# Two-layer hybrid encoder: GpSimd makes the low parts of nine attention weight tiles a layer, the first A head's weights are turned by VectorE and transfers, V's second block is scaled by VectorE

## The chip, the core and the metric

The kernel runs on one core of a Trainium2 chip. The time is that of the device, in microseconds (us), from the start to the end of one execution; the median of several executions counts. The engines in the text are TensorE (PE in the profile: matrix products, and PEld, its weight loads), VectorE (DVE), ScalarE (ACT), GpSimd (POOL) and SyncE (SP), which here only starts transfers. SBUF is the on-chip memory that all of them read and write, PSUM the accumulators that TensorE writes. Each engine runs its own instructions in order.

## The reference

The kernel computes a trunk of two layers over 256 tokens (S) of width 1024 (D), all in float32:

```python
for l in range(2):
    x = x + 0.5 * swiglu(rms_norm(x, ffn1_norm[l]), ffn1_w_gate[l], ffn1_w_up[l], ffn1_w_down[l])   # width 2816
    h = rms_norm(x, mix_norm[l])
    qa, ka, va, qb, kb, vb = split(h @ w_in[l])         # 512, 128, 128, 512, 512, 512 columns
    out_a = windowed_gqa_sink(qa, ka, va, sink[l])      # 8 query heads of 64, 2 key/value heads, window +-128
    out_b = differential_attention(qb, kb, vb, lam)     # 4 heads of two softmaxes, values 128 wide
    out_b = rms_norm(out_b, diff_subln[l]) * (1 - lam_init)
    x = x + concat(out_a, out_b) @ w_out[l]
    x = x + 0.5 * swiglu(rms_norm(x, ffn2_norm[l]), ffn2_w_gate[l], ffn2_w_up[l], ffn2_w_down[l])
return rms_norm(x, final_norm)
```

Both attentions add a bias that grows with the distance (ALiBi); A's softmax has a learned sink logit in its denominator; B's weights are softmax 1 minus lambda times softmax 2.

## The kernel before

**Products in three parts.** A float32 value is split into a high part (the value cast to fp32r, a shorter float) and a low part (the value minus the high part). Each product is made of three: activations' high by weights' high, low by high, high by low. ScalarE casts the high parts, VectorE subtracts for the low ones.

**The stream of weights.** `specs` lists all weight tiles in the order of use. SP's queue brings each into one of six buffers `raw`; `emit_split(i, j)` makes the high and low tiles (both named `w`) of half j of tile i, in one of seven pairs of buffers. Tiles in the set `fine` are split in two pieces of 128x512, so that one half tile is two casts and two subtractions. `ahead` and `weights` run this some halves ahead of use. In the attention a layer has 13 tiles: 0 and 1 are the keys of B, 2 and 3 its queries, 4 the keys and values of A, 5 and 6 its queries, 7 and 8 the values of B, 9 to 12 the output projection.

**The attention (`mix`).** Its steps are written in the order: keys and queries of B, `soft_b` for heads 0 and 1, keys and values of A, `soft_b` for heads 2 and 3, queries of A, `soft_a(0)` and `soft_a(1)`, the values of B with `soft_a(2)` and `soft_a(3)` between their two weight tiles. One call of `soft_a` does two query heads of A that share one query tile, an A head pair; the prediction calls each call's work an A head, and calls 0 and 1, or 2 and 3, a pair. It makes 12 small score products on TensorE, four minima with the bias on VectorE (`negm`), four exponentials on ScalarE, and four multiplications by 1/sum (`ra`) on VectorE:

```python
w_ = e[:, t, a * 256:a * 256 + 256]
dve.tensor_scalar_mul(w_, w_, r[:, 2 * t + a:2 * t + a + 1])
```

The weights then have tokens on the partitions, and the value products need the keys there. `keys_first` turns them: per half of the keys, four 128x128 transposes on TensorE into a bank of PSUM, and one copy of 128x512 out of it, the first half by ScalarE, the second by VectorE. `aT[0]` and `aT[1]` are the turned tiles of B's heads 0, 1 and 2, 3; `pT[0..3]` are those of A's four calls. `vB` holds the values of B: each block of 128 tokens comes out of PSUM by one multiplication with the norm factor `r`, which GpSimd computes (a power).

**Another way to turn.** `Blocks` turns a tile without TensorE: `take` is a VectorE transpose within blocks of 32x32 (one for each 128 rows), `move` four transfers on SP's queue that place the blocks, `turned` the view in which the operand then lies: 32 elements in a run. Before the change only the norms use it.

**What sets the order.** Up to the values of B a scheduler orders each engine's instructions in the attention, by its own estimates and by priority (`urgent` raises it). From the products of V with the weights on (`kept[0] = True`) the engines run in the order written: the 32 products of B's values (eight take `aT[0]`, eight `aT[1]`, then the same for the second block of tokens), `values_a(0)`, the turning of A's calls 2 and 3, `norm_b`, which starts B's head norm, `values_a(1)`, the output projection. In the feed-forward parts the order is written out by hand in `ORDER`; GpSimd adds some weights to others there while transferring them.

## Time and profile before

| | us |
|---|---|
| median of 3 runs (906.02 to 906.24) | 906.07 |
| the profiled execution | 906.06 |
| its span in the profile | 904.3 |
| TensorE busy | 895.8 (99%) |
| its weight loads busy | 753.7 (83%) |
| VectorE busy | 738.9 (82%) |
| ScalarE busy | 562.0 (62%) |
| GpSimd busy | 52.8 (6%) |

The span runs from the first to the last instruction of the profile; the profiled execution's time is 1.76 us more. The granted clock of TensorE is 0.998 of full speed. Layer 0's attention lies between about 185 and 255 us of the span. In rows of the timeline the first number is the start in us and the second the time until the last of the group ended; then come engine, line (L80 for nearly all, since one helper issues them), operation, output<-inputs, shape and count. `ps` is a PSUM bank, `s` one of the 14 general buffers of 128x1024. In brackets stands a wait ahead of the row, and what ended it. In rows of groups the numbers behind the bar are busy time in us, mean ns of one, and idle time ahead.

### The profile page before, as it was taken

How to read it: one execution, taken by the hardware profiler on the slowest of the kernel's cores; microseconds unless marked ns; L12 is line 12 of the kernel's file. 1: busy time of each engine (PE TensorE's matmuls, PEld its weight loads, DVE VectorE, ACT ScalarE, POOL GpSimd, SP SyncE). 2: the span in 40 equal slices, each digit the busy share in tenths (PEclk: the TensorE clock that was granted, in tenths of full speed). 3: DMA queues.
4: the chain of work that ended last, by engine and by line, in shares of the span. 5: the costliest groups of instructions: out<-in, count | busy, mean ns of one | idle time of the engine just before them, and what ended most of it. 6: DMA issues, size and time to landing. Idle time of an engine off the chain costs nothing.

```text
span 904.3 us, 12641 instructions
## 1 busy us (share of the span) xinstructions
PE 895.8 (99%) x4514; PEld 753.7 (83%) x4514; DVE 738.9 (82%) x1110; ACT 562.0 (62%) x913; POOL 52.8 (6%) x72
## 2 busy tenths in 40 slices
PE   9999999999999999999999999999999999999997
PEld 7878888899878888888888888888998888888886
DVE  6689997879977798987768978888798768978883
ACT  6766655567746675665575664654686485665661
POOL 0411000000000010000000000000000000000001
PEclk9999999999999999999999999999999999999999
DMA  9989999766526979999769899996752478799921
GB/s 341 318 248 320 331 242 329 221 169 184 159 73 191 269 211 309 315 239 311 236 173 282 199 330 278 297 289 181 199 184 94 117 207 274 197 347 278 296 65 46
DMA packets 137664, 211.36 MB, mean 234 GB/s; under 512 B 5759, under 2 KB 56001, under 8 KB 137601
## 3 DMA queue, kind: packets, MB, share of 16 engines
q1 hardware_dynamic: 123840, 184.05, 62.0%
q0 software_dynamic: 12928, 25.46, 16.3%
q10 hardware_dynamic: 832, 1.05, 0.3%
q8 instruction: 35, 0.57, 0.3%
q14 instruction: 29, 0.23, 0.1%
HBM read 192.71 MB, written 1.05 MB: 214 GB/s over the span
## 4 chain that ended last, share of the span: by engine, by line
PE 95%; DVE 2%; ACT 2%; issue 1%; POOLq 0%; POOL 0%; DVEq 0%; ACTq 0%
PE ps L80 95%; DVE w L80 1%; ACT w L80 1%; ACT s L80 1%; DVE s L80 0%; DVE tmp L80 0%; ACT tmp L80 0%; ACT L80 0%; DVE xk L80 0%; POOLq L1225 0%; POOL rf L80 0%; DVEq L1225 0%; ACT junk L80 0%; ACTq L80 0%; DVE rf L80 0%
## 5 line engine op out<-in xcount | busy, mean ns | idle before, releaser
L80 PE MATMUL ps<-w,s 128*128 128x512 f32 (+1 forms) x2994 | 681.5, 388 | 0.4 <-DVE s L80 0.4
L80 PEld LDWEIGHTS ps<-w,s 128*128 128x128 f32 x2994 | 558.8, 188 | 116.8 <-issue 0.8
L80 DVE TENSOR_TENSOR w<-raw,w 128x1024 fp32r<-128x1024 f32 (+1 forms) x416 | 434.2, 1085 | 76.3 <-ACT w L80 72.3
L80 ACT CAST w<-raw 128x1024 fp32r<-128x1024 f32 (+1 forms) x416 | 377.3, 942 | 170.2 <-PE ps L80 146.1
L80 PE MATMUL ps<-s,w 128*128 128x256 f32 x672 | 83.8, 285 | 0.0
L80 PEld LDWEIGHTS ps<-s,w 128*128 128x128 f32 x672 | 81.7, 191 | 1.2
L80 PE MATMUL ps<-w,q 128*128 128x512 f32 x288 | 69.3, 390 | 0.1
L80 PEld LDWEIGHTS ps<-w,q 128*128 128x128 f32 x288 | 53.9, 188 | 11.7 <-issue 0.5
L80 ACT ACTIVATE s<-s,gcol 128x256 fp32r<-128x256 f32 (+1 forms) x64 | 27.0, 497 | 42.4 <-DMA s<-s 42.4
L80 DVE STREAM_TRANSPOSE s<-s 128x512 f32<-128x512 f32 (+1 forms) x48 | 46.2, 1000 | 0.0
L80 POOL DMA_DIRECT2D raw<-in_ffn_w_up_dram x16 | 21.0, 1314 | 398.1 <-DVE ms L80 145.0
L80 ACT CAST s<-s 128x256 fp32r<-128x256 f32 x88 | 29.3, 403 | 11.1 <-DMA s<-s 11.0
L80 ACT ACTIVATE s<-s,negm 128x256 f32<-128x256 f32 x64 | 31.9, 500 | 6.6 <-DVE negm L80 6.3
L80 DVE TENSOR_TENSOR s<-s,s 128x256 fp32r<-128x256 f32 x88 | 31.5, 419 | 4.7 <-ACT s L80 4.7
L80 ACT ACTIVATE tmp<-ps,r 128x512 f32<-128x512 f32 (+1 forms) x40 | 24.9, 643 | 13.3 <-PE ps L80 12.6
L80 ACT CAST q<-tmp 128x512 fp32r<-128x512 f32 x20 | 12.3, 617 | 30.0 <-DVE tmp L80 30.0
L80 DVE TENSOR_TENSOR xk<-xk,ps 128x512 f32<-128x512 f32 x21 | 14.3, 682 | 18.1 <-PE ps L80 18.1
L80 DVE SCALAR_TENSOR_TENSOR s<-s,gcol,s 128x256 fp32r<-128x256 f32 x40 | 16.8, 483 | 10.7 <-ACT s L80 10.6
L80 PE MATMUL ps<-w,v 128*128 128x512 f32 x96 | 23.4, 390 | 0.5 <-DVE w L80 0.5
L80 DVE STREAM_TRANSPOSE s<-xk 128x512 f32<-128x512 f32 x20 | 22.0, 1101 | 0.7
L80 ACT ACTIVATE tmp<-tmp,r 128x512 f32<-128x512 f32 x8 | 5.8, 724 | 26.1 <-DVE tmp L80 26.1
L80 PEld LDWEIGHTS ps<-w,v 128*128 128x128 f32 x96 | 17.9, 188 | 4.6 <-DVE w L80 0.9
(117 smaller groups left out, 419.4 us busy)
## 6 DMA issues: line engine op xcount, KB each, us to landing
raw<-in_ffn_w_down_dram SPq DMA_DIRECT2D x44, 1024.0 KB, 8.2
raw<-in_ffn_w_gate_dram SPq DMA_DIRECT2D x39, 1024.0 KB, 5.7
raw<-in_ffn_w_up_dram SPq DMA_DIRECT2D x39, 1024.0 KB, 7.1
raw<-in_ffn_w_up_dram POOLq DMA_DIRECT2D x16, 1024.0 KB, 9.4
s<-s SPq DMA_DIRECT2D x120, 128.0 KB, 3.0
raw<-in_w_in_dram SPq DMA_DIRECT2D x14, 1024.0 KB, 6.4
raw<-in_ffn_w_gate_dram POOLq DMA_DIRECT2D x8, 1024.0 KB, 9.6
raw<-in_ffn_w_gate_dram SPq DMA_DIRECT2D x8, 512.0 KB, 4.7
```

What stands on the lines that cost most here:

```text
L80: ins = issue(*a, **k)
```

## The change

1. `slow` names tiles 2 to 10 of each layer's attention. Their 36 low pieces of 128x512 are subtracted by GpSimd instead of VectorE.
2. A's first call, `soft_a(0)`, is multiplied by 1/sum on ScalarE instead of VectorE, and is turned by `keys_turned(0)`: two VectorE transposes and four transfers instead of eight TensorE transposes and two copies. Its tile is then read in runs of 32 elements.
3. The copies of `aT[1]` are both VectorE's, instead of one by ScalarE and one by VectorE.
4. The second block of `vB` comes out of PSUM by VectorE instead of ScalarE.
5. `norm_b` starts ahead of `values_a(0)`.

```diff
-    fine = {2, 3}
+    fine, slow = {2, 3}, set()
...
-            dve.tensor_tensor(l_, r_, f(h_), op=ALU.subtract)
+            (pool if i in slow else dve).tensor_tensor(l_, r_, f(h_), op=ALU.subtract)
...
+        slow.update(mixed + i for i in (2, 3, 4, 5, 6, 7, 8, 9, 10))
...
-                    dve.tensor_scalar_mul(w_, w_, r[:, 2 * t + a:2 * t + a + 1])
+                    if c in (0,):
+                        act.mul(w_, w_, r[:, 2 * t + a:2 * t + a + 1])
+                    else:
+                        dve.tensor_scalar_mul(w_, w_, r[:, 2 * t + a:2 * t + a + 1])
...
-        def keys_first(pick):
+        def keys_first(pick, copies=(act.copy, dve.tensor_copy)):
...
-                (act.copy if kc == 0 else dve.tensor_copy)(out_[:, kc], tsl)
+                copies[kc](out_[:, kc], tsl)
...
+        def keys_turned(c):
+
+            turn = Blocks(by_block=False)
+            for t in range(2):
+                turn.take(p_a[c][:, t], t)
+            turn.move()
+            return turn.turned().rearrange("p (a k) y j -> p a k y j", a=2)
...
-            return keys_first(lambda kc, i: a_b[2 * hp + i // 2][:, i % 2, kc * P:(kc + 1) * P])
+            return keys_first(lambda kc, i: a_b[2 * hp + i // 2][:, i % 2, kc * P:(kc + 1) * P],
+                              [dve.tensor_copy] * 2 if hp else (act.copy, dve.tensor_copy))
...
             if k0 == 0:
+                pT = [keys_turned(0)]
                 p_a += [soft_a(2, qA1[0]), soft_a(3, qA1[1])]
         with urgent():
-            for t in range(2):
-                act.activation(vB[:, t], vsl[t], AF.Copy, scale=norm.r[:, t:t + 1])
+            act.activation(vB[:, 0], vsl[0], AF.Copy, scale=norm.r[:, 0:1])
+            dve.tensor_scalar_mul(vB[:, 1], vsl[1], norm.r[:, 1:2])
         aT.append(keys_first_b(1))
-        pT = [keys_first_a(c) for c in range(2)]
+        pT.append(keys_first_a(1))
...
-                        pe.matmul(o[j][f0, 0:S], lhsT=vA[:, kc, f0], rhs=pT[2 * cp + j][:, kc, a * 256:a * 256 + 256],
+                        pe.matmul(o[j][f0, 0:S], lhsT=vA[:, kc, f0], rhs=pT[2 * cp + j][:, a, kc],
...
+        normed = norm_b()
+        next(normed)
         values_a(0)
         pT += [keys_first_a(c) for c in (2, 3)]
-        normed = norm_b()
-        next(normed)
```

VectorE at the end of layer 0's softmaxes, before: `es`, `ra` and the `s` that `ra` multiplies belong to `soft_a(2)` and `soft_a(3)`, `w<-raw` is a low piece, and `s_450` is `aT[1]`; the other copies are A's turned tiles.

```order
L80 TENSOR_TENSOR es_2466<-negm_2457,snk 128x4
L80 TENSOR_TENSOR w_2523<-raw_2087,w_2522 128x512
L80 TENSOR_TENSOR es_2500<-negm_2491,snk 128x4
L80 TENSOR_TENSOR w_2523<-raw_2087,w_2522 128x512
L80 COPY s_450_2550<-ps_2557 128x512
L80 TENSOR_TENSOR ra_2469<-den_a_1673,es_2466 128x4
L80 COPY s_453_2563<-ps_2570 128x512
L80 RECIPROCAL ra_2469<-ra_2469 128x4
L80 COPY s_456_2576<-ps_2583 128x512
L80 TENSOR_SCALAR s_435_2456<-s_435_2456,ra_2469 128x256 x4
```

The same place of VectorE in the changed kernel, where `v` is `vB`'s second block and `s_452` is `aT[1]`:

```order
L80 TENSOR_TENSOR es_2508<-negm_2499,snk 128x4
L80 TENSOR_TENSOR ra_2477<-den_a_1673,es_2474 128x4
L80 TENSOR_TENSOR ra_2511<-den_a_1673,es_2508 128x4
L80 RECIPROCAL ra_2477<-ra_2477 128x4
L80 RECIPROCAL ra_2511<-ra_2511 128x4
L80 TENSOR_SCALAR s_437_2464<-s_437_2464,ra_2477 128x256
L80 TENSOR_SCALAR v_2401<-ps_2403,r_1787 128x512
L80 TENSOR_SCALAR s_437_2464<-s_437_2464,ra_2477 128x256 x3
L80 TENSOR_SCALAR s_443_2498<-s_443_2498,ra_2511 128x256 x4
L80 TENSOR_TENSOR w_2531<-raw_2087,w_2530 128x512 x2
L80 COPY s_452_2558<-ps_2559 128x512
L80 COPY s_452_2558<-ps_2565 128x512
```

VectorE's one copy of `aT[1]` stood ahead of the multiplications of `soft_a(2)` and `soft_a(3)`; now it has two, and both stand behind all eight of these, `vB`'s second block and two low pieces.

GpSimd from the last feed-forward transfer before layer 0's attention, in the changed kernel; `r` is the attention's norm factor:

```order
L80 DMA raw_720<-in_ffn_w_gate_dram 128x4x512
L80 TENSOR_TENSOR w_1675<-raw_1465,w_1674 128x512 x2
L80 TENSOR_TENSOR w_1681<-raw_1465,w_1680 128x512 x2
L80 TENSOR_TENSOR w_1687<-raw_1524,w_1686 128x512 x2
L80 TENSOR_TENSOR r_1787<-ms_1784,mhalf 128x2
L80 TENSOR_TENSOR w_1807<-raw_1524,w_1806 128x512 x2
L80 TENSOR_TENSOR w_1827<-raw_1578,w_1826 128x512 x2
```

Before, `r` came right behind the transfer, and nothing but `rb` of `norm_b` followed in the attention; now six low pieces stand ahead of `r`, and 30 between `r` and `rb`.

TensorE ahead of the value products of B, before; `ident` marks a transpose, `s_412` and `s_418` are the weights of A's calls 0 and 1:

```order
L80 MATMUL ps_2557<-ident,s_384_2133 128x128 x2
L80 MATMUL ps_2557<-ident,s_389_2162 128x128 x2
L80 MATMUL ps_2564<-ident,s_412_2334 128x128 x4
L80 MATMUL ps_2570<-ident,s_412_2334 128x128 x4
L80 MATMUL ps_2577<-ident,s_418_2368 128x128 x4
L80 MATMUL ps_2583<-ident,s_418_2368 128x128 x4
L80 MATMUL ps_2593<-v_2401,s_422_2388 128x128 x4
L80 MATMUL ps_2593<-v_2401,s_450_2550 128x128 x4
```

And now:

```order
L80 MATMUL ps_2565<-ident,s_384_2133 128x128 x2
L80 MATMUL ps_2565<-ident,s_389_2162 128x128 x2
L80 MATMUL ps_2572<-ident,s_418_2368 128x128 x4
L80 MATMUL ps_2578<-ident,s_418_2368 128x128 x4
L80 MATMUL ps_2588<-v_2401,s_422_2388 128x128 x4
L80 MATMUL ps_2588<-v_2401,s_452_2558 128x128 x4
```

The eight transposes of A's first call are gone, and so there is less between the transposes into `aT[1]`'s banks and the products that read it.

More of the change, by code (lines that the diff above doesn't have):

```diff
@@ L1004, in keys_first @@
                     pe.transpose(tsl[:, i * P:(i + 1) * P], pick(kc, i), ident)
-                (act.copy if kc == 0 else dve.tensor_copy)(out_[:, kc], tsl)
+                copies[kc](out_[:, kc], tsl)
             return out_
+        def keys_turned(c):
[4 more added lines that the diff above has]
+            return turn.turned().rearrange("p (a k) y j -> p a k y j", a=2)
         def keys_first_b(hp):
-            return keys_first(lambda kc, i: a_b[2 * hp + i // 2][:, i % 2, kc * P:(kc + 1) * P])
+            return keys_first(lambda kc, i: a_b[2 * hp + i // 2][:, i % 2, kc * P:(kc + 1) * P],
+                              [dve.tensor_copy] * 2 if hp else (act.copy, dve.tensor_copy))
         def keys_first_a(c):
-            return keys_first(lambda kc, i: p_a[c][:, i % 2, (i // 2) * 256 + kc * P:(i // 2) * 256 + (kc + 1) * P])
+            t_ = keys_first(lambda kc, i: p_a[c][:, i % 2, (i // 2) * 256 + kc * P:(i // 2) * 256 + (kc + 1) * P])
+            return t_.rearrange("p k (a y j) -> p a k y j", a=2, j=32)
         aT = [keys_first_b(0)]
```

## The prediction

> **What bounds the kernel now.** I read the page first, then the waits of TensorE and the chain, and then the order of time of layer 0's attention, where every edit lies.

> ```profile
> span 904.3 us, 12641 instructions
> PE 895.8 (99%) x4514; PEld 753.7 (83%) x4514; DVE 738.9 (82%) x1110; ACT 562.0 (62%) x913; POOL 52.8 (6%) x72
> PE ps L80 <- DVE tmp L80: 1.4, 1, 1.4
> 76.94 816.92 PE ps L80 x4155
> ```

> TensorE is busy for all but 8.5 us. Its longest wait is 1.4 us, at the start, and the chain is one unbroken piece of TensorE work from 76.94 us to 893.86. The profiled execution took 906.06 us, 1.76 more than its span and level with the median of 906.07. So relief of another engine is worth nothing by itself. The time falls by the TensorE work that goes, and rises by every wait that the change puts into that piece. The other engines have little room there: the timeline shows VectorE with hardly a gap from 200 to 250 us.

> **TensorE work that goes.**

> ```profile
> 207.23 0.50 PE L80 MATMUL ps<-s,q 64*128 64x256 f32 x4
> 211.57 1.45 PE L80 MATMUL ps<-s,q 64*128 64x256 f32 x20
> 215.17 1.69 PE L80 MATMUL ps<-s,q 64*128 64x256 f32 x24
> 228.70 0.50 PE L80 MATMUL ps<-s,q 64*128 64x256 f32 x4
> 244.37 2.78 PE L80 MATMUL ps<-ident,s 128*128 128x128 f32 x24
> 246.99 3.74 PE L80 MATMUL ps<-v,s 128*128 128x128 f32 x32
> 250.65 1.95 PE L80 MATMUL ps<-s,vA 128*64 128x256 f32 x16
> ```

> The 24 transposes before B's value products take 246.99 - 244.37 = 2.62 us, 0.109 each. Eight of them, the first A head's, go: 0.87 us. The new order also issues two groups of 24 score products in one piece that are now cut into 4 and 20: 0.50 + 1.45 - 1.69 = 0.26 each, 0.5 together. That is 1.37 us a layer and 2.74 us for both; the second layer repeats the first. With nothing else this gives 903.3 us. The value products of A then read half of their moving operand in runs of 32 elements instead of 256. No row shows TensorE reading so. I take nothing; if these 8 of 16 took twice their 0.12 us it would be 1.0 us a layer.

> **The wait that comes: B's second weight tile.** The products at 246.99 need both blocks of V at once and, after the first 8 of 32 (3.66 / 32 = 0.114 each, so 0.91 us later), the tile of B's heads 2 and 3. In the changed kernel they could start at 246.99 - 1.37 = 245.62, and would need that tile's first half at 246.53 and its second at 246.76. Now ScalarE copies one half and VectorE the other, and VectorE's copy stands ahead of the last A heads' scaling:

> ```profile
> 231.34 0.48 DVE L80 CUSTOM_DVE_ANT_0 s<-ps,distA,nsnk 128x256 f32<-128x256 f32 x1
> 237.75 2.19 DVE L80 TENSOR_SCALAR s<-s,ra 128x256 f32<-128x256 f32 x8
> 239.86 0.48 DVE L80 CUSTOM_DVE_ANT_0 s<-ps,distA,nsnk 128x256 f32<-128x256 f32 x1
> 245.66 0.68 DVE L80 COPY s<-ps 128x512 f32<-128x512 f32 x1
> 230.84 0.58 ACT L80 COPY s<-ps 128x512 f32<-128x512 f32 x1
> 231.87 0.51 ACT L80 ACTIVATE s<-s,negm 128x256 f32<-128x256 f32 x1 [0.45 <-DVE negm L80]
> 237.12 0.28 ACT L80 ACTIVATE es<-es 128x4 f32<-128x4 f32 x2
> 237.31 1.12 ACT L80 CAST w<-raw 128x512 fp32r<-128x512 f32 x2
> 242.37 0.67 ACT L80 ACTIVATE v<-ps,r 128x512 f32<-128x512 f32 x1
> 190.54 1.71 ACT L80 ACTIVATE s<-s,gcol 128x256 fp32r<-128x256 f32 x4 [5.89 <-DMA s<-s]
> 36.98 2.05 DVE L80 STREAM_TRANSPOSE s<-s 128x512 f32<-128x512 f32 x2
> ```

> In the new order both copies are VectorE's and stand behind the whole softmax of A heads 2 and 3, V's second block and two halves of a low part. I follow the chain in two pieces.

> First piece, from the first A pair's score minimum to the second's. Without VectorE's low parts ahead of it the first minimum could start when its scores are there: 228.70 - 0.26 + about 1.0 for the first twelve products and their latency, 229.4. Then: 0.53 to the first exponential (231.34 to 231.87); eight exponentials at 0.49 a start (3.93) and a copy (0.47); two small exponentials and two casts (1.24); the four new multiplications by 1/sum on ScalarE, as the 190.54 row (1.71); VectorE's two 32x32 transposes that wait for them (2.05); half a low part (0.6). Together 10.5 us, so the second pair's minimum starts at 239.9. Now it starts at 239.86: what the low parts free, the new steps in the chain use up.

> Second piece, from 239.9: 0.5 to the exponentials, 3.93 for eight and 0.57 for V's first block between them (5.0); small exponentials (0.28) and VectorE's small operations (0.37); one multiplication (0.26), V's second block (0.6), seven more multiplications (1.85; eight take 2.19), two halves of low parts (1.2), the copy (0.68): 10.24 us. The second copy adds 0.6. The halves land at 250.1 and 250.75. V's second block lands at 246.5, inside the same wait. TensorE needs the second half at 246.76: it waits 4.0 us a layer.

> Without anything more the sum is 906.06 + 2 x 4.0 - 2.74 = 911.3 us.

> **GpSimd's low parts and VectorE.**

> ```profile
> L80 DVE TENSOR_TENSOR w<-raw,w 128x512 fp32r<-128x512 f32 x22 | 14.3, 685 | 0.9 <-ACT w L80 0.7
> L80 DVE SCALAR_TENSOR_TENSOR s<-s,rc 128x256 f32<-128x256 f32 x8 | 3.4, 480 | 0.0
> L80 DVE TENSOR_TENSOR q<-tmp,q 128x512 fp32r<-128x512 f32 x3 | 2.1, 685 | 0.0
> L80 DVE TENSOR_TENSOR s<-tmp,s 128x512 fp32r<-128x512 f32 x2 | 1.3, 683 | 0.0
> L80 DVE SCALAR_TENSOR_TENSOR rc<-rc,nlam,den_b 128x2 f32<-128x2 f32 x4 | 0.8, 213 | 0.0
> L80 DVE TENSOR_TENSOR s<-tmp,s 128x256 fp32r<-128x256 f32 x1 | 0.4, 408 | 0.0
> L80 POOL TENSOR_TENSOR xk<-xk,s 128x512 f32<-128x512 f32 x2 | 2.6, 1300 | 45.4 <-ACT tmp L80 45.4
> 42.56 0.90 DVE L80 TENSOR_TENSOR q<-tmp,q 128x512 fp32r<-128x512 f32 x1 [0.69 <-ACT q L80]
> 43.52 2.36 DVE L80 TENSOR_TENSOR w<-raw,w 128x1024 fp32r<-128x1024 f32 x2
> 42.47 0.45 POOL L80 TENSOR_TENSOR distB<-distB 128x128 f32<-128x128 f32 x1
> L80 POOL TENSOR_TENSOR distB<-distB x2: 449/688/927, 42.5 to 45.3; 128x128 f32<-128x128 f32 x2
> ```

> The first six rows are VectorE's from 200 to 231 us. A half low part of 128x512 takes VectorE 0.685 us (0.6 to the next start), and took GpSimd 1.30 in the nearest row. There are 36 halves a layer, 46.8 us of GpSimd, from 185.5 on.

> The two work against each other. At 42.56 VectorE's q, which reads two SBUF tiles, started while GpSimd ran a product of two SBUF tiles, and took 0.90 us instead of 0.69. The other such product of GpSimd, at 45.3, met VectorE's low part of the 43.52 row and took 0.93 instead of 0.45. In the first case VectorE lost 0.21 us to a product that had begun 0.09 us earlier: GpSimd held it for 0.31 of its 0.45, all but 0.14. By that a half low part holds VectorE's two-input operations for up to 1.16 us.

> [...] With 1.30 for 1.16 as the hold the estimate would be about 3 us above mine.

> Between 200 and 231 us 18 such operations stay with VectorE (8 + 3 + 2 + 4 + 1). One that arrives at any time while GpSimd works waits half of 1.16, 0.58; one that arrives behind another, with GpSimd in line, waits the whole. GpSimd holds 36 x 1.16 = 42 us of some 60, so a mean of 0.4 is the low end; 0.85 is the high one; I take 0.7: 12.6 us. What VectorE is spared there is 21 halves (one of the 22 is cut by the window's edge) at 0.6, also 12.6. So the first A minimum comes where it comes now, at 231.3, and not at 229.4: 1.9 us later, and TensorE waits for the q and scores ahead of it. Two more such waits in the pieces above, q's second pair and a low half, add 1.4. That is 3.3 us a layer (0.8 at a mean of 0.4, some 6 at 0.85), and 7.3 with the 4.0.

> **The sum.** 906.06 + 2 x 7.3 - 2.74 = 917.9; I say 918.0 us.

> **What stays hidden.**

> ```profile
> 185.51 3.66 DVE L80 TENSOR_TENSOR w<-raw,w 128x512 fp32r<-128x512 f32 x6
> 194.10 0.73 POOL L80 TENSOR_TENSOR r<-ms,mhalf 128x2 f32<-128x2 f32 x1 [68.78 <-DVE ms L80]
> 198.68 0.59 PE L80 MATMUL ps<-dg,ones 128*128 128x256 f32 x2
> s<-s SPq DMA_DIRECT2D x120, 128.0 KB, 3.0
> 245.76 0.37 SPq L186 DMA_DIRECT2D raw<-in_ffn_w_gate_dram  x1
> ```

> GpSimd's r, on which the whole attention waits, now stands behind six low halves: 6 x 1.30 = 7.8 us from 185.51 is 193.3, just ahead of r at 194.10, and r's first user on TensorE comes at 198.68. Covered; were the halves 2 us each, r would come at 197.5 and about 1 us would show. The turned tile's four transfers land 3.0 us after the transposes, some 7 us before A's value products. On SP's queue they stand ahead of one weight load, issued at 245.76 now; the transposes are done by then. Cost nothing; that load is five tiles ahead of its use, so a slip of a few us stays hidden too.

> **The rivals.**
> No contention (0.16): the two rows above have other causes or other sizes, GpSimd runs beside VectorE, and only the copy's wait is left: 911.3 us. Against it stands that both engines' rows show the loss at the same moment, each against the other.

> Faster (0.10): the copies of B's second tile land by 246.8 all the same, because VectorE gets 4 us ahead in the attention, and only the saved TensorE work counts: 903.3 us. It needs the second pair's minimum to start by about 236, ahead of the end of its own scores in the present trace, so little speaks for it. It decides when the second copy lands before 246.76.

> No change (0.03): the wait is as small as the saving, 1.4 us a layer.

> GpSimd becomes the bound (0.07): at 1.9 us a half, as the 45.3 row doubled, V's eight halves come slower than the 1.43 us in which TensorE uses one up, fall 3.8 us behind, and TensorE waits for low parts: 918.0 + 2 x 3.8 = 925.6 us. For it speaks that VectorE's operations hold GpSimd up as well; against it the six tiles of lead.

> **How the numbers follow.** The forecast case has 0.64. Its ends are 906.06 + 2 x 4.8 - 2.74 = 912.9 at a mean wait of 0.4, and 906.06 + 2 x 10.0 - 2.74 = 923.3 at 0.85. The range reaches down to the case without contention with an error of 0.8 us a layer in its chain, 909.5, and up to 924. The faster case and most of the GpSimd case are left out. A measurement of this kernel tells 0.2%, 1.8 us, from no change. Faster has 0.10, the same 0.03, slower 0.87.

> **What would show it.** In the changed profile TensorE's waits should name VectorE before the products of V with B's tiles, 3 to 6 us a layer, with two VectorE copies side by side just ahead of their second group. A further 2 to 4 us should lie at the first A pair's scores. Low halves on GpSimd should take about 1.3 us each and up to half more, and VectorE's two-input operations of the attention should be longer than now, up to about 1.8 us, while those that read PSUM keep their length. Transposes should fall by 16. If VectorE's two-input operations keep their length, the contention step is wrong. If TensorE has no wait before B's value products, the chain is wrong. If it waits for GpSimd, the third rival holds.

## The result, and the profile after

The changed kernel takes 926.5 us (median of 4 runs, 925.32 to 927.19), the kernel before 906.05 on the same chip: 1.0223 times as long, interval 1.0211 to 1.0236. The forecast was 918.0 in a range of 909.5 to 924.0. The sign was right; the size was not: 20.4 us were added, where 12 were forecast.

The head of the page of the changed kernel, and TensorE's waits (engine and tile that wait, engine and tile waited for; us in total, times, longest us):

```profile
span 925.4 us, 12626 instructions
PE 903.1 (98%) x4498; PEld 760.3 (82%) x4498; DVE 730.2 (79%) x1036; ACT 561.5 (61%) x915; POOL 151.2 (16%) x144
PE ps L80 <- DVE s L80: 5.8, 3, 2.7
PE ps L80 <- ACT q L80: 3.3, 2, 1.7
PE ps L80 <- DVE v L80: 3.1, 2, 1.6
PE ps L80 <- DVE q L80: 2.1, 2, 1.1
PE ps L80 <- DVE tmp L80: 1.4, 1, 1.4
```

The profiled execution took 927.19 us, 21.1 more than the one before. The waits are 16.0 us with a small one that is not shown, and were 2.3: 13.7 of the 21.1. The other 7.3 are in TensorE's busy time, 903.1 for 895.8, although it has 16 products fewer. Where they come from shows in the timeline of TensorE in layer 0's attention:

```profile
229.72 0.39 PE L80 MATMUL ps<-s,q 64*128 64x256 f32 x2 [1.66 <-ACT q L80]
231.18 2.72 PE L80 MATMUL ps<-s,q 64*128 64x256 f32 x22 [1.08 <-DVE q L80]
233.83 1.97 PE L80 MATMUL ps<-ident,s 128*128 128x128 f32 x8
235.45 6.70 PE L80 MATMUL ps<-w,s 128*128 128x512 f32 x24
243.69 5.74 PE L80 MATMUL ps<-w,s 128*128 128x512 f32 x24
249.26 1.91 PE L80 MATMUL ps<-ident,s 128*128 128x128 f32 x16
251.01 0.39 PE L80 MATMUL ps<-v,s 128*128 128x128 f32 x2
252.95 0.94 PE L80 MATMUL ps<-v,s 128*128 128x128 f32 x6 [1.56 <-DVE v L80]
256.59 5.33 PE L80 MATMUL ps<-v,s 128*128 128x128 f32 x24 [2.70 <-DVE s L80]
261.86 1.95 PE L80 MATMUL ps<-s,vA 128*64 128x256 f32 x16
```

Two things are to be seen. There are two pairs of waits: 1.66 and 1.08 us ahead of A's first scores, for the two parts of q, and 1.56 and 2.70 ahead of B's value products, for V's second block and for the copies of B's second tile. And behind each pair the same products take longer: 24 products with V's weights take 6.70 us at 235.45 and 5.74 at 243.69; 24 of B's value products take 5.33, where 32 took 3.74 before, 2.8 for 24. The stretches of 2 us there say why (columns: busy time and count of PE, PEld, DVE, ACT and POOL, then the granted clock of TensorE, the transfers' share, GB/s):

```profile
228.00:230.00 2.00, 0.34 (x3) 0.19 (x2) 1.31 (x4) 1.11 (x3) 2.00 (x2) 1.00 0.00 0
232.00:234.00 2.00, 2.00 (x19) 1.78 (x18) 1.35 (x7) 1.39 (x4) 2.00 (x3) 0.50 0.93 362
238.00:240.00 2.00, 2.00 (x11) 1.64 (x10) 0.62 (x4) 0.71 (x3) 0.01 (x1) 1.00 0.63 238
258.00:260.00 2.00, 2.00 (x11) 2.00 (x11) 0.49 (x1) 0.60 (x1) 0.00 (x0) 0.50 1.02 386
```

The granted clock is halved for 6.83 us at each pair in layer 0, from within the second wait on, and for 3.41 and 6.83 us in layer 1. These 23.9 us hold 4.7 us in which TensorE stood idle; of the rest one half is lost, 9.6 us. The busy time says the same. Of the 2.74 us of work that was to go, 2.3 went: the 16 transposes and, in each layer, 0.26 for one group of 24 scores; the second group was to come in one piece and came as 2 and 22, with a wait between them. The work that stayed took 7.3 + 2.3 = 9.6 us longer.

VectorE from 200 to 231 us, the groups that answer to those of before (busy us, mean ns), and GpSimd's low pieces of the whole program:

```profile
L80 DVE SCALAR_TENSOR_TENSOR s<-s,rc 128x256 f32<-128x256 f32 x8 | 8.6, 1118 | 0.1
L80 DVE TENSOR_TENSOR q<-tmp,q 128x512 fp32r<-128x512 f32 x3 | 4.5, 1494 | 0.7 <-ACT q L80 0.7
L80 DVE SCALAR_TENSOR_TENSOR rc<-rc,nlam,den_b 128x2 f32<-128x2 f32 x4 | 2.4, 608 | 0.1
L80 DVE CUSTOM_DVE_ANT_0 s<-ps,distB 128x256 f32<-128x256 f32 x16 | 5.8, 415 | 0.1
L80 POOL TENSOR_TENSOR w<-raw,w 128x512 fp32r<-128x512 f32 x72 | 98.1, 1399 | 124.6 <-ACT w L80 68.0 <-DVE xk L80 56.6
```

VectorE's operations with two inputs in SBUF went from 480 to 1118 ns and from 685 to 1494, even the one of 128x2 from 213 to 608. The minima, which read PSUM, kept their length (421 before, 415 now).

### The profile page after: what moved, and what is told of

It reads as the page before. It is cut to its first block, busy times and chain, and to the rows that moved or that the text cites. A ratio compares the mean times of both kernels' runs of the same rounds, so it can differ in the third digit from the quotient of the medians.

```text
span 925.4 us, 12626 instructions
## 1 busy us (share of the span) xinstructions
PE 903.1 (98%) x4498; PEld 760.3 (82%) x4498; DVE 730.2 (79%) x1036; ACT 561.5 (61%) x915; POOL 151.2 (16%) x144
## 4 chain that ended last, share of the span: by engine, by line
PE 87%; DVE 9%; ACT 2%; issue 1%; POOLq 0%; POOL 0%; DVEq 0%; ACTq 0%
PE ps L80 87%; DVE s L80 5%; DVE w L80 1%; ACT s L80 1%; DVE q L80 1%; DVE tmp L80 1%; DVE rc L80 1%; ACT w L80 1%; DVE ra L80 0%; ACT q L80 0%; ACT tmp L80 0%; DVE v L80 0%; ACT v L80 0%; DVE xk L80 0%; POOLq L1240 0%
## 5 line engine op out<-in xcount | busy, mean ns | idle before, releaser
L80 PE MATMUL ps<-w,s 128*128 128x512 f32 (+1 forms) x2994 | 683.3, 389 | 0.4 <-DVE s L80 0.4
L80 PEld LDWEIGHTS ps<-w,s 128*128 128x128 f32 x2994 | 560.3, 188 | 117.3 <-issue 0.8
L80 ACT CAST w<-raw 128x1024 fp32r<-128x1024 f32 (+1 forms) x416 | 376.0, 941 | 162.6 <-PE ps L80 137.2
L80 DVE TENSOR_TENSOR w<-raw,w 128x1024 fp32r<-128x1024 f32 (+1 forms) x344 | 387.3, 1167 | 71.5 <-ACT w L80 68.9
L80 POOL TENSOR_TENSOR w<-raw,w 128x512 fp32r<-128x512 f32 x72 | 98.1, 1399 | 124.6 <-ACT w L80 68.0
L80 POOL DMA_DIRECT2D raw<-in_ffn_w_up_dram x16 | 21.0, 1314 | 408.3 <-DVE ms L80 153.7
L80 PE MATMUL ps<-s,w 128*128 128x256 f32 x672 | 83.0, 284 | 0.0
L80 PEld LDWEIGHTS ps<-s,w 128*128 128x128 f32 x672 | 81.5, 192 | 0.8
L80 PE MATMUL ps<-w,q 128*128 128x512 f32 x288 | 69.3, 390 | 0.0
L80 PEld LDWEIGHTS ps<-w,q 128*128 128x128 f32 x288 | 54.0, 188 | 11.6 <-issue 0.4
L80 ACT ACTIVATE s<-s,gcol 128x256 fp32r<-128x256 f32 (+1 forms) x64 | 27.0, 497 | 43.0 <-DMA s<-s 43.0
L80 DVE STREAM_TRANSPOSE s<-s 128x512 f32<-128x512 f32 (+1 forms) x52 | 50.4, 1008 | 0.0
L80 ACT CAST s<-s 128x256 fp32r<-128x256 f32 x88 | 29.3, 402 | 14.2 <-DMA s<-s 14.2
L80 DVE TENSOR_TENSOR s<-s,s 128x256 fp32r<-128x256 f32 x88 | 31.5, 418 | 7.9 <-ACT s L80 7.9
L80 ACT ACTIVATE s<-s,negm 128x256 f32<-128x256 f32 x64 | 31.8, 498 | 9.6 <-DVE negm L80 9.3
L80 ACT ACTIVATE tmp<-ps,r 128x512 f32<-128x512 f32 (+1 forms) x40 | 24.8, 642 | 13.3 <-PE ps L80 12.7
L80 DVE SCALAR_TENSOR_TENSOR s<-s,gcol,s 128x256 fp32r<-128x256 f32 x40 | 16.8, 483 | 19.1 <-ACT s L80 18.9
L80 ACT CAST q<-tmp 128x512 fp32r<-128x512 f32 x20 | 12.3, 616 | 29.0 <-DVE tmp L80 29.0
L80 POOL DMA_DIRECT2D raw<-in_ffn_w_gate_dram x8 | 10.3, 1286 | 117.5 <-DVE w L80 117.5
L80 DVE TENSOR_TENSOR q<-tmp,q 128x512 fp32r<-128x512 f32 x20 | 20.1, 1004 | 9.7 <-ACT q L80 9.7
L80 DVE TENSOR_TENSOR xk<-xk,ps 128x512 f32<-128x512 f32 x21 | 14.3, 679 | 16.4 <-PE ps L80 16.4
L80 PE MATMUL ps<-w,v 128*128 128x512 f32 x96 | 23.4, 391 | 0.3 <-DVE w L80 0.3
## 6 DMA issues: line engine op xcount, KB each, us to landing
s<-s SPq DMA_DIRECT2D x128, 128.0 KB, 3.2
```

What stands on the lines that cost most here:

```text
L80: ins = issue(*a, **k)
```

## The experiments

My theory after the result: GpSimd's subtractions hold up VectorE, the scheduler's new order puts the copies of B's second tile late, and every wait of TensorE that this makes is followed by work at half the clock. The rivals: the loss is in the turned tile and the copies, or TensorE's products are slower for another cause than its standing idle.

**All low parts back on VectorE (dve_low).** The rest of the change stays.

```diff
-        slow.update(mixed + i for i in (2, 3, 4, 5, 6, 7, 8, 9, 10))
```

> The changed kernel with all low parts back on VectorE; the rest of the change stays. Theory (GpSimd's low parts lengthen VectorE's two-input operations, the late copies of B's second tile add a wait, and each wait is followed by TensorE work at a lower clock): the waits at A's first scores are gone, VectorE's two-input operations keep 0.48 and 0.69 us. VectorE has 2.15 us more than before in front of the second copy, so TensorE waits 1.7 us a layer there, loses about 1.5 to the clock, and saves 1.37: about 910 us. Rival (the loss is in the turned tile and the copies, not in GpSimd): waits of 4 us or more stay and the time is 918 us or more.

Measured: 906.15 us, 0.9999 times before, interval 0.999 to 1.0009. The whole loss hangs on the GpSimd step. TensorE waits 0.63 us a layer for the second copy, not 1.7, and the clock stays up (1.0 in the run's mean):

```profile
246.72 1.28 PE L80 MATMUL ps<-v,s 128*128 128x128 f32 x10
248.63 2.72 PE L80 MATMUL ps<-v,s 128*128 128x128 f32 x22 [0.63 <-DVE s L80]
```

That I expected more has a cause in the order. With the low parts on VectorE, the scheduler puts both copies ahead of the multiplications by 1/sum; with them on GpSimd it puts them behind. The step that I saw as a relief of VectorE also chose the bad place.

**Only the low parts to GpSimd (low_only).** The kernel before with the line above added, and the subtraction on GpSimd for these tiles.

> The kernel before with only the 36 low pieces a layer moved to GpSimd. Theory: the waits at A's first scores are those of the changed kernel, 2.7 us a layer, with about 3 us a layer of lower clock behind them; VectorE's copy of B's second tile now stands behind the multiplications, for up to 1 us of wait: 906 + 2 x (2.7 + 3 + 0.5) = 918 us. Rival (GpSimd's work costs little, the copies and the turned tile cost the rest): under 909 us.

Measured: 919.33 us, 1.0143 times before (1.0126 to 1.016). Alone the step costs 13.0 us. The time is near the 918 expected, but partly by luck: the waits are 8.5 us longer in all than before, where 6.4 were expected, and TensorE's busy time 4.8, where 6 were expected.

```profile
230.55 0.39 PE L80 MATMUL ps<-s,q 64*128 64x256 f32 x2 [1.11 <-ACT q L80]
232.02 2.23 PE L80 MATMUL ps<-s,q 64*128 64x256 f32 x22 [1.09 <-DVE q L80]
255.04 2.72 PE L80 MATMUL ps<-v,s 128*128 128x128 f32 x22 [1.57 <-DVE s L80]
L80 DVE SCALAR_TENSOR_TENSOR s<-s,rc 128x256 f32<-128x256 f32 x8 | 8.6, 1121 | 0.1
```

Its parts do not add up: 13.0 alone, nothing for the rest alone, 20.4 together. Late as VectorE then is, the turned tile and V's block come on top of the wait for the copies, and behind these longer waits (1.56 and 2.70 us) the clock was at 0.50. In low_only, behind 0.55 us for V's block and 1.57 for the copies, the 22 products take 2.72 us, as they do in dve_low behind 0.63.

**Only the turned tile (turn_only).** The kernel before with `act.mul` for A's first call, `keys_turned(0)`, and the operand's view.

> The kernel before with only A's first call scaled by ScalarE and turned by VectorE and transfers. Theory: VectorE has 0.95 us more ahead of its copy of B's second tile, TensorE waits about 0.5 us a layer there and saves 1.37, so 904.5 us, or 905.5 if the short wait also lowers the clock. Rival (reading the turned tile in runs of 32 slows A's value products by 1 us a layer or more): those products take over 2.4 us in place of 1.95, and the time is 906 us or more.

Measured: 912.15 us, 1.0064 times before (1.0049 to 1.0079). Neither theory had this. The turned tile's two transposes delay the second pair's minima, so ScalarE's exponentials, and V's second block stands behind some of these on ScalarE:

```profile
248.17 0.95 PE L80 MATMUL ps<-v,s 128*128 128x128 f32 x6 [1.86 <-ACT v L80]
249.32 4.38 PE L80 MATMUL ps<-v,s 128*128 128x128 f32 x24 [0.20 <-ACT s L80]
253.64 1.95 PE L80 MATMUL ps<-s,vA 128*64 128x256 f32 x16
```

2.06 us of waits and 4.38 - 2.8 = 1.6 by which the 24 products are longer, less 0.87: 2.8 a layer, 5.6 of the 5.9 measured. In dve_low VectorE takes that block out of PSUM and the wait for it is gone; that this move alone does it is not shown, since dve_low also has both copies on VectorE and `norm_b` earlier. The last row settles one point: A's value products still take 1.95 us with runs of 32.

**TensorE kept busy in the waits (warm).** The changed kernel with:

```diff
+        def fill(n):
+            for _ in range(n):
+                pe.transpose(osl[1][:, 0:P], ident, ident)
+        fill(14)
         for t in range(2):
             for h in range(HB):
+                if t == 0 and h == 2:
+                    fill(24)
```

> The changed kernel with filler transposes on TensorE, into a bank that is not yet in use: 14 ahead of B's value products and 24 ahead of those that need B's second tile, 4.1 us inside the waits there. They change no result. Theory (the slower products behind a wait come from the clock that falls while TensorE stands idle): the 24 products behind the wait take 2.8 us in place of 5.3, the granted clock stays near 1.0 there, and the time falls by about 5 us to 921.5 us though the fillers do no useful work. Rival (the products are slower from another cause, such as where their operands come from): they stay at 5.3 us and the time stays at 926.5 us or rises.

Measured: 923.35 us, 1.0185 times before (1.017 to 1.02); 3.1 us less than the changed kernel with 76 products more.

```profile
253.37 2.78 PE L80 MATMUL ps<-ident 128*128 128x128 f32 x24
256.24 3.32 PE L80 MATMUL ps<-v,s 128*128 128x128 f32 x24
256.00:258.00 2.00, 1.80 (x14) 1.46 (x13) 1.38 (x3) 0.19 (x1) 0.00 (x0) 1.00 0.62 123
```

The 24 products take 3.32 us in place of 5.33, at a clock of 1.00 in place of 0.50. The operands are the same, so it was the idle time that lowered the clock there. From the first filler to the last value product it is 8.8 us a layer, where the changed kernel takes 10.8 from the first value product. The gain in all is 3.1 us, not 5: the 24 products still take 0.5 us over 2.8, and what the waits at A's scores cost, where there are no fillers, varies without a change there (the 22 scores behind them took 2.72 and 1.62 us in the two layers of the changed kernel, 2.36 and 2.72 here).

**Made waits (gaps, gaps2).** The kernel before with a pause ahead of B's value products and of the output projection's second half:

```diff
+    z = const.tile([P, 256], F32, name="z")
...
+    def pause(bank_, n):
+        for i in range(2):
+            pe.transpose(bank_[:, 0:P], z[:, 0:P], ident)
+            if i == 0:
+                for _ in range(n):
+                    pool.memset(z, 0.5)
...
+        pause(osl[1], (2, 8)[l])
...
+        pause(accs[1][1], (4, 12)[l])
```

That is gaps; gaps2 has (5, 7) and (6, 10).

> The kernel before with a made wait of TensorE at two places of each layer: a transpose, so many memsets of 128x256 on GpSimd that wait for it (2, 4, 8, 12), and a transpose that waits for these, into a bank not yet in use; the results are not touched. The places are ahead of B's value products (2 in layer 0, 8 in layer 1) and ahead of the output projection's second half (4 in layer 0, 12 in layer 1). Theory (the clock falls after a wait): behind the short waits, under 0.7 us, the products keep their length; behind those of 1.5 us and more they are slower for some us, and 1 to 3 us are lost on top of each. Rival (the slower products of the changed kernel have another cause): the time grows by the waits alone, and the products behind them take what they take in the kernel before.

> The kernel with made waits once more, with 5 and 7 memsets ahead of B's value products and 6 and 10 ahead of the output projection's second half, which gives waits of about 2.1, 2.8, 2.6 and 3.9 us. Theory (the clock halves once TensorE has stood idle long enough, between 2.0 and 3.1 us in one piece by the first run with made waits): the granted clock stays at 1.0 behind 2.1 us and is 0.5 for some 3 to 6 us behind 3.9; the two between tell where the change lies. Rival (the loss grows evenly with the wait): some loss behind each.

Measured: 923.65 us (2 runs, 1.0188 times before, 1.017 to 1.0207) and 924.69 (one run). First the value products of gaps behind 0.80 and 3.14 us, then those of gaps2 behind 1.99 and 2.74, with its wait of 2.33 between them, and four stretches of 3.41 us of gaps2, two at the wait of 1.99 and two at that of 2.33:

```profile
248.49 3.74 PE L80 MATMUL ps<-v,s 128*128 128x128 f32 x32
698.44 0.37 PE L80 MATMUL ps<-ident,z 128*128 128x128 f32 x1 [3.14 <-POOL z L80]
698.60 5.36 PE L80 MATMUL ps<-v,s 128*128 128x128 f32 x32
```

```profile
249.12 0.33 PE L80 MATMUL ps<-ident,z 128*128 128x128 f32 x1 [1.99 <-POOL z L80]
249.28 5.37 PE L80 MATMUL ps<-v,s 128*128 128x128 f32 x32
275.17 0.33 PE L80 MATMUL ps<-ident,z 128*128 128x128 f32 x1 [2.33 <-POOL z L80]
701.14 6.53 PE L80 MATMUL ps<-v,s 128*128 128x128 f32 x32
246.19:249.60 3.41, 1.42 (x13) 1.19 (x12) 3.23 (x12) 2.20 (x7) 1.64 (x5) 1.00 0.85 253
249.60:253.01 3.41, 3.41 (x18) 3.41 (x17) 1.07 (x4) 0.00 (x0) 0.00 (x0) 0.50 0.14 55
270.08:273.49 3.41, 2.76 (x13) 2.00 (x11) 2.43 (x4) 1.96 (x2) 0.47 (x2) 1.00 0.16 63
273.49:276.90 3.41, 1.73 (x8) 1.47 (x9) 3.33 (x3) 0.13 (x1) 1.40 (x5) 1.00 0.22 42
```

Behind 0.80 us the 32 products take 3.74, as in the kernel before; behind 1.99 they lose 1.6 us, behind 2.74 2.8, behind 3.14 1.6. The waits of 3.81 us (gaps2) and 4.54 (gaps) are followed by 3.4 and 6.0 us of work at half the clock, a loss of 1.7 and 3.0. But behind 2.33 us, and behind 1.96 in gaps, the clock stayed at 1.00. No one length of a wait separates the two cases here. The expectation of one such length did not hold, nor did that of a loss which grows with the wait.

More is seen when the granted clock of the changed kernel is read closely. While there is work left, it falls four times, at 230.72, 254.61, 688.10 and 708.58 us, and stays at 0.50 for 6.83, 6.83, 3.41 and 6.83 us. The last three of these stretches begin 7, 134 and 140 times 3.413 us behind the first, so all the changes of the clock there lie on one grid of 3.41 us. The trace read in the windows of this grid, the one ahead of each fall and those at half the clock:

```profile
227.31:230.72 3.41, 1.14 (x9) 0.73 (x7) 2.73 (x4) 2.52 (x7) 3.41 (x4) 1.00 0.12 13
230.72:234.13 3.41, 2.95 (x24) 2.73 (x25) 2.67 (x10) 2.60 (x7) 3.41 (x3) 0.50 0.84 295
234.13:237.55 3.42, 3.42 (x13) 3.03 (x12) 3.42 (x12) 3.41 (x14) 3.42 (x3) 0.50 0.43 119
251.20:254.61 3.41, 1.13 (x8) 0.75 (x7) 3.14 (x13) 1.84 (x7) 0.00 (x0) 1.00 0.01 2
254.61:258.02 3.41, 1.43 (x6) 1.33 (x7) 3.12 (x6) 0.00 (x0) 0.00 (x0) 0.50 0.28 43
258.02:261.44 3.42, 3.42 (x18) 3.42 (x18) 0.69 (x1) 0.60 (x1) 0.00 (x0) 0.50 0.69 263
684.69:688.10 3.41, 1.79 (x24) 1.56 (x24) 2.72 (x6) 3.19 (x6) 3.41 (x4) 1.00 0.56 167
688.10:691.51 3.41, 3.41 (x16) 2.98 (x13) 3.41 (x10) 2.81 (x10) 3.41 (x3) 0.50 0.43 153
705.17:708.58 3.41, 1.37 (x10) 0.98 (x8) 2.90 (x12) 2.08 (x7) 0.00 (x0) 1.00 0.02 7
708.58:711.99 3.41, 1.20 (x5) 1.10 (x6) 3.35 (x7) 0.00 (x0) 0.00 (x0) 0.50 0.18 22
711.99:715.41 3.42, 3.42 (x18) 3.42 (x18) 0.69 (x1) 0.60 (x1) 0.00 (x0) 0.50 0.80 285
```

What came next went with TensorE's busy time in the window. The four windows ahead of a fall hold 1.14, 1.13, 1.79 and 1.37 us of it; every other window of this grid at full clock, up to 920 us, holds 2.29 or more, and the clock stayed up behind it. At half the clock, the windows with 2.95, 1.43 and 1.20 us busy were followed by another at half, the four that were busy throughout by the full clock. In gaps2 a window with 1.42 us was followed by half the clock, and one with 1.73 was not, so the busy time alone does not settle what lies near 1.75.

The rows fit this. The wait of 1.99 us lay inside one window and left 1.42 us busy; the end of a window cut that of 2.33 into 0.65 and 1.68. The wait of 2.74 still ran when the clock fell (its mean from 700 to 702 us is 0.54), and the loss of 2.8 us is that of two windows; the 1.6 behind the longer wait of 3.14 is that of one. So waits of 1.96 to 3.14 us cost from nothing to 2.8 us beyond their length here, by where they fell in these windows, and no kernel here chose that.

**GpSimd's work without relief (pool_read).** The kernel before; GpSimd subtracts the same 36 pieces a layer into a scratch tile while VectorE makes them as well.

```diff
             dve.tensor_tensor(l_, r_, f(h_), op=ALU.subtract)
+            if i in slow:
...
+                pool.tensor_tensor(d_, r_, f(h_), op=ALU.subtract)    # d_: scratch
```

> The kernel before, where GpSimd makes the 36 low pieces a layer of the changed kernel a second time, into a scratch tile that nobody reads; VectorE still makes all of them, in nearly the order of before. Theory (GpSimd's subtractions hold VectorE's two-input operations): these take 1.1 us and more in place of 0.48 and 0.69, VectorE, full as it is, falls behind by 10 to 30 us a layer, and the time is 930 us or more. Rival (the engines do not hold each other up; the loss comes from the new order): VectorE's operations keep their length and the time stays under 910 us.

Measured: 968.88 us, 1.0686 times before (1.0668 to 1.0704). VectorE from 200 to 250 us, and GpSimd:

```profile
L80 DVE TENSOR_TENSOR w<-raw,w 128x512 fp32r<-128x512 f32 x21 | 28.9, 1420 | 0.0
L80 DVE CUSTOM_DVE_ANT_0 s<-ps,distB 128x256 f32<-128x256 f32 x16 | 5.7, 414 | 0.0
L80 POOL TENSOR_TENSOR junk<-raw,w 128x512 f32<-128x512 f32 x72 | 111.7, 1552 | 163.8 <-ACT w L80 150.0 <-issue 9.3
```

The order is nearly that of before, so the 62.7 us are the two engines' hold on each other and what follows from it, TensorE's waits (the longest 5.4 us) and the lower clock (0.88 on average from 190 to 260 us): 685 ns became 1420, and the minima, which read PSUM, stayed at 414.

**The copies ahead (copies_first).** The changed kernel with priority for the turning of B's second tile:

```diff
-        aT.append(keys_first_b(1))
+        with urgent():
+            aT.append(keys_first_b(1))
```

> The changed kernel with its low parts on GpSimd, and a higher priority for the turning of B's second tile: VectorE's two copies of it now stand ahead of the multiplications by 1/sum, V's second block still among them. Theory (waits and a lower clock behind each): the 2.70 us of wait for the copies are gone, the wait for V's second block stays at 1 to 2 us, the waits and the lower clock at A's first scores stay as they are: 926.5 - 2 x (2.7 + about 1) = 919 us. Rival (the loss is all in GpSimd's contention, the place of the copies is of no account): within 2 us of 926.5.

Measured: 916.94 us, 1.0116 times before (1.0102 to 1.013), 9.6 under the changed kernel. The wait for the copies is gone, that for V's block stays. Behind it the same 30 products take 3.62 us in layer 0 and 5.24 in layer 1, 1.6 longer:

```profile
252.48 3.62 PE L80 MATMUL ps<-v,s 128*128 128x128 f32 x30 [1.55 <-DVE v L80]
701.64 5.24 PE L80 MATMUL ps<-v,s 128*128 128x128 f32 x30 [2.04 <-DVE v L80]
```

So the place of the copies and what followed from it were nearly half of the loss. At A's first scores of layer 0 the waits are the same as in the changed kernel (1.73 and 1.08 for 1.66 and 1.08), but the 24 products behind take 5.70 us in place of 6.70, since the clock was low for about 3.4 us there (means of 0.97, 0.50, 0.68 and 1.00 in the four stretches of 2 us from 230 on) and not for 6.83.

**Fewer low parts on GpSimd (s11, half11), and none between the copies (low_last).** The three try for a version that beats both kernels.

```diff
 s11
-        slow.update(mixed + i for i in (2, 3, 4, 5, 6, 7, 8, 9, 10))
+        slow.update(mixed + i for i in (11,))
 half11: the same for the second half of tile 11 alone
 low_last: no GpSimd; the second half of tile 11 is split behind the turning of B's second tile
-            w = weights()
+            w = weights(held=k0 == 4)
...
+        i_v = w.i
         aT.append(keys_first_b(1))
+        kept[0] = True
+        ahead(2 * i_v + 1 + HALVES)
+        kept[0] = False
```

> The changed kernel with another choice of tiles for GpSimd: only the third tile of the output projection (number 11), whose four low pieces stand among VectorE's last steps of the softmaxes, where hardly a two-input operation is left to hold up. Theory (GpSimd costs where VectorE has two-input operations, and helps where it has none): VectorE's copies of B's second tile come 2 us earlier than with all low parts on VectorE, the wait of 0.63 us a layer there is gone, and TensorE keeps the 0.87 us a layer of the eight transposes: 906.2 - 1.7 = 904.5 us. Rival (any low part on GpSimd costs more than it frees): 907 us or more.

> As s11, but GpSimd makes only the second half (two low pieces a layer) of that weight tile. In s11 the first half fell beside the four multiplications by 1/sum, which took 3.22 us in place of 1.15; the second half falls beside VectorE's work on PSUM. Theory (GpSimd holds VectorE's operations from SBUF to SBUF, not those that read PSUM): the multiplications take 1.15 us again, V's second block and both copies land as TensorE needs them, the wait of 0.63 us a layer that was left with all low parts on VectorE is gone: 906.2 - 2 x 0.6 to 0.9 = 904.7 us. Rival (any piece on GpSimd here costs what it frees): 906 us or more.

> As dve_low (all low parts on VectorE, the rest of the change stays), with the second half of tile 11 split behind the turning of B's second tile, so that VectorE's two copies of it follow each other and the two low pieces stand behind them. Theory (with VectorE undisturbed, the 0.63 us of wait for the second copy is the low piece that stands between the copies): the wait is gone and TensorE keeps the 0.87 us a layer of the eight transposes: 906.2 - 2 x 0.6 = 905.0 us, or 904.5 with the whole saving. Rival (another wait of the same length is next in line): 906 us or more.

Measured: s11 906.62 us (1.0004, 0.9995 to 1.0013), half11 906.69 (1.0008, 0.9999 to 1.0017), low_last 905.44 (0.9994, 0.9984 to 1.0003). The first two missed. First VectorE's four multiplications by 1/sum in dve_low and in s11, then, in half11, one addition of 128x4:

```profile
238.45 1.15 DVE L80 TENSOR_SCALAR s<-s,ra 128x256 f32<-128x256 f32 x4
```

```profile
237.79 3.22 DVE L80 TENSOR_SCALAR s<-s,ra 128x256 f32<-128x256 f32 x4
```

```profile
245.84 1.07 DVE L80 TENSOR_TENSOR es<-negm,snk 128x4 f32<-128x4 f32 x1
246.84 1.87 DVE L80 COPY s<-ps 128x512 f32<-128x512 f32 x3
```

Two low pieces on GpSimd lengthened the multiplications, which have one tile from SBUF as input, by 2.1 us, and TensorE waits 0.65 us for V's second block, which stands behind them. In half11 the addition, 0.17 us in dve_low, met GpSimd's piece and took 1.07, and the copies stood behind it; TensorE still waits 0.58 us for them. In low_last, as expected, TensorE's list has no wait over 0.2 us left but the 1.4 at the start; the 0.7 us that it is ahead is not clear of the measurement. No version here is measurably faster than the kernel before.

## Why the prediction was wrong

**The step that failed** is the first line of the sum: "The time falls by the TensorE work that goes, and rises by every wait that the change puts into that piece." TensorE's remaining work was counted at the length that it has in the profile before, where the granted clock is 1.00 as long as TensorE works. That profile has no wait of over 1.4 us ahead of a product, so no row of it shows a product behind a longer one. It does show that the clock falls, at its end, behind the last product, which ends at 898.15:

```profile
900.00:902.00 2.00, 0.00 (x0) 0.00 (x0) 0.82 (x2) 0.66 (x1) 0.00 (x0) 0.57 0.36 125
```

It fell at 900.27, 2.1 us after the last product; the mean of 0.998 comes from there. The prediction did not read it, and put what follows a wait at nothing. The term measures 9.6 us. With it, with the waits of 13.7 and with the 2.3 us of work that went the sum is 906.06 + 13.7 + 9.6 - 2.3 = 927.1; the profiled execution took 927.19. That idle time is the cause is shown by warm and by the made waits.

**The waits were nearly right in size.** 14.6 us were forecast, 13.7 came. The wait at A's first scores was forecast at 3.3 us a layer and is 2.74; the one ahead of B's value products at 4.0 and is 4.26. Its inside is other than forecast: 1.56 us of it are for V's second block, which was to land inside the wait for the copies. That the second came out so close is partly luck. VectorE's first copy landed at 256.5 us, 3.1 later than forecast (250.1 + 3.3), mainly because the chain's first piece took 13.3 us and not 10.5: ScalarE's cast in it waited 1.35 us for TensorE, and the transposes stood behind four multiplications of the other call. TensorE, at its lower clock, came to the value products 2.1 us later than forecast (251.0, for 245.6 + 3.3), and the two delays largely cancel.

**Contention was right**, and so was its mean: the operations of 200 to 231 us lost (1118 - 480) x 8 + (1494 - 685) x 3 + (608 - 213) x 4 ns = 9.1 us on 15 of the 18, 0.61 each, for the 0.7 taken. That operations with two inputs in SBUF are held came as forecast, and so did the unchanged length of the minima, which read PSUM (421 ns before, 415 in the changed kernel). Too narrow was my reading that only the former are held: the multiplications by 1/sum, with one such input, took 3.22 us in place of 1.15 in s11.

**The chain was right for a part of the reason only.** The copies stood where the order showed them. That they stand there because of the GpSimd step, and not of the step that gives both to VectorE, came out with dve_low.

**What was called hidden was hidden.** TensorE waits for GpSimd nowhere, so r and the low parts come in time; the transfers of the turned tile and its runs of 32 cost nothing (1.95 us for the 16 products as before); 16 transposes went. Of the two groups of 24 scores the first came in one piece of 1.69 us; the second did not, as its second half of q came late.

**The rivals.** No contention is refuted by pool_read, GpSimd as the bound by the list of waits. The time alone refutes faster and no change. The case nearest in time, GpSimd as the bound at 925.6, had the wrong cause.

## What to carry to other kernels

Where one engine is busy without a break, price a wait at its length and at the slower work behind it: here 13.7 us of waits cost 23.3, and single waits of up to 1.57 us only their length. If a wait cannot be removed, useless work that keeps the engine busy in it may still pay: in warm it took 3.1 us off. Giving work to GpSimd paid nowhere here; it held up VectorE's operations from SBUF to SBUF (480 ns became 1118), and not the minima, which read PSUM (421 and 415), and an operation on four columns that met it took 1.07 us. When a scheduler sets the order, a moved operation also moves others: compare the order with and without that one step before judging the rest of a change.
